# The low part of the weights: a subtraction on VectorE, or a transfer that adds onto the negated high part

## The chip, the cores and the metric

One core of a Trainium2 chip runs the whole program in one launch. The metric is the device time of one execution in microseconds (us). All inputs and outputs lie in HBM.

## What is computed

Three transformer blocks in a row on one sequence of 512 tokens by 1024 channels, in float32. Every block is a mixer and a gated feed-forward of width 2816:

```python
def reference(x, ...):
    x = first_block(x, ...)    # sparse attention (compressed, selected, windowed) + spatial gating, conv feed-forward
    x = second_block(x, ...)   # 2 layers: attention over selected keys + differential attention, swiglu feed-forward
    return third_block(x, ...) # state space branch + delta rule branch, swiglu feed-forward

# the feed-forward of the second block (each layer) and of the third
gate = jnp.einsum('bsd,df->bsf', h2, w_gate[layer])
up = jnp.einsum('bsd,df->bsf', h2, w_up[layer])
x = x + jnp.einsum('bsf,fd->bsd', jax.nn.silu(gate) * up, w_down[layer])
```

Nearly all of the arithmetic is products of activations with weights: the input projections, the output projections and the four feed-forwards (one in the first block, two in the second, one in the third).

## The kernel before

Activations are kept with channels on the 128 partitions and the 512 tokens along the free dimension. A product runs in the matmul format `float32r`, which rounds its operands, so each operand is split into a high part `hi` (the value rounded to `float32r`) and a low part `lo` (the value minus `hi`), and a product is three matmuls: `hi*hi`, `hi*lo`, `lo*hi` (`mm3`, L350 to L352).

Weights come in pieces of 128 partitions by up to 1024 columns (512 KB), 8 tiles of 128 rows of the contraction. `load_piece` (L277) makes one piece: SP issues the load into a raw buffer (`wraw`, `WR` = 4 buffers, L281); ACT copies it with rounding into `whi` (L283); DVE subtracts, `wlo = wraw - whi` (L284). `whi` and `wlo` have `WS` = 3 buffers each. There are 528 pieces in the program: 176 for the gate and up projections (`wup`), 118 for the input projections (`win`), 128 for the down projections (`wdn`: each row of output blocks is one piece of 1024 columns and one of 384, as half of the width is 11 tiles), 56 for the output projections (`wout`, 48 of them 512 columns wide), and some tens of others.

The consumers are `lin_steps` (L299), which takes a piece and issues 24 matmuls (8 tiles by three), each of 128 by 512, and `tok_steps` (L316), which uses the weights as the moving operand. `swiglu` (L1606) makes one tile of 128 channels of the feed-forward: a product with a gate piece, DVE multiplies by the row scale `rbc`, ACT applies Silu, POOL multiplies by `rbc` once more (L1612), a product with an up piece, DVE multiplies the two (L1614) and the result is split again (L291, L292). `out_proj` (L1628) does the output and down projections: per block of 128 channels DVE adds the product to `x`, and ACT and DVE prepare the next normalization.

The framework orders each engine's instructions itself: each engine then runs its own list in order, and tiles with several buffers let a list run ahead as far as buffers come free. SP's list has the loads. POOL's list has elementwise work (L436, L875, L877, L1612 and others), small dependent steps of a triangular system in the third block (L1298, L1303), and six transfers of its own (L1287, L1305, L1310). The rotary embedding (`rope`, L868) exchanges halves by transfers issued from ACT (L874).

The lines that are replaced:

```python
hi, lo = (self.t([P, 1024], tag=tg, bufs=self.WS, dt=F32R, name=tg)[:, :n] for tg in ("whi", "wlo"))
nc.scalar.copy(hi, raw)
nc.vector.tensor_tensor(lo, raw, hi.bitcast(F32), op=ALU.subtract)
```

Of the kernel before, what the change touches and what calls it, by code (L numbers as in the profile page):

```python
# [12 lines left out]
F32 = mybir.dt.float32  # L13
F32R = mybir.dt.float32r
I32 = mybir.dt.int32
AF = mybir.ActivationFunctionType
ALU = mybir.AluOpType
# [3 lines left out]
P = 128  # L21
# [9 lines left out]
# ---------------------------------------------------------------- host layout  # L31
def kpieces(w):
    """[K, M] -> [M/128, 128, K/128 * 128]: one block of columns per row, the contraction on partitions."""
    k, m = w.shape
    a = w.reshape(k // P, P, m // P, P).transpose(2, 1, 0, 3)
    return np.ascontiguousarray(a).reshape(m // P, P, k)


def kmajor(w):
    """[K, N] -> [128, K/128 * N]."""  # L40
    k, n = w.shape
    return np.ascontiguousarray(w.reshape(k // P, P, n).transpose(1, 0, 2)).reshape(P, -1)


def colvec(v):
    """[n * 128] -> [128, n]."""
# [24 lines left out]
def prep(i):  # L71
# [22 lines left out]
    # block 1  # L94
# [43 lines left out]
    # block 2  # L138
# [31 lines left out]
    # block 3  # L170
# [27 lines left out]
# ---------------------------------------------------------------- device code  # L198
class Build:
    def __init__(self, tc, aps, offs, ctx):  # L200
        self.tc, self.nc, self.aps, self.offs = tc, tc.nc, aps, offs
        self.ctx = ctx
        self.uid = 0
        self.sb = ctx.enter_context(tc.tile_pool(name="sb", bufs=1))
# [15 lines left out]
    def t512(self, dt=F32, name="t"):  # L220
        """A [128, 512] slot, taken in program order and given back with free()."""
# [15 lines left out]
    def set_ring(self, **kinds):  # L237
        """Slots that short-lived tiles of a kind go round; 0 gives them back."""
# [13 lines left out]
    def banks(self, **kinds):  # L252
        """Which PSUM banks each kind of product goes round."""
# [22 lines left out]
    # weights: one DMA of [128, n <= 1024], then the exact two-part split  # L276
    def load_piece(self, ap):  # L277
        nc = self.nc
# [7 lines left out]

    def split(self, src, name="s", tiles=None):
        """src [128, n] F32 (SBUF or PSUM) -> hi, lo."""
# [6 lines left out]
    def lin_T(self, ap, xs, tag="mm", piece=None):  # L295
        """ap [128, K] (one block of 128 output rows); xs: list of (hi, lo) per k-tile -> PSUM [128, 512]."""
        return last_of(self.lin_steps(ap, xs, tag, piece))

    def lin_steps(self, ap, xs, tag="mm", piece=None):  # L299
        """lin_T, a k-tile a step; the last step gives the result."""  # L300
# [16 lines left out]
    def tok_steps(self, ap, n, xs, done, wide=1):  # L317
        """ap [128, 8 * n]: tokens on partitions, PSUM [128, n] per token tile to done(tt, ps)."""
# [22 lines left out]
    def scaled(self, o, scale, name):  # L341
        """o * scale in two parts."""
# [4 lines left out]
    def mm3(self, out, w, x, start=True, stop=True):  # L347
        """out (+)= w.T @ x, either operand in two parts."""
# [5 lines left out]
    def scores(self, q, k, qt, masks, mx, sm):  # L354
        """Per half: exp(max - (q.k + mask)) with its row sums; q carries the turned sign."""
# [19 lines left out]
    def turned(self, t, qt):  # L375
        """[queries, keys] -> the blocks of keys on partitions, [128, block, 128 queries]."""
# [10 lines left out]
    def rsqrt(self, y, v, pool=False):  # L387
        """y = v ** -0.5 on small [128, n] tiles; v is SBUF and positive."""
# [17 lines left out]
    def bcast_cols(self, col_of_tt, tag="at"):  # L406
        """[128 tokens, 128 (broadcast)] stationary per token tile -> PSUM [128, 512] rows."""
# [5 lines left out]
    def bcast_pairs(self, cols, tag="at"):  # L413
        """cols [128 tokens, 4, 2] -> PSUM [128 = (2, 64), 512]."""
# [4 lines left out]
    # sums of squares of the residual stream, and what follows from them  # L419
# [19 lines left out]
    def col_sums(self, *accs):  # L439
        """-> PSUM [128 tokens, 4]: sums over the partitions."""  # L440
# [9 lines left out]
    def stat_end(self, st):  # L450
        """-> [128 tokens, 4]: 1 / rms"""
# [13 lines left out]
    def norm_in(self, x, g, hi, lo):  # L465
        """hi + lo = x * g, g a per-partition column."""
# [6 lines left out]
    # ------------------------------------------------------------ block 1  # L473
    def block1(self, x, B, first, g_next, stats):
# [36 lines left out]
        # the overlapping windows of the compressed keys and values, position pairs on partitions  # L511
# [99 lines left out]
        # relative bias strips, sign turned: strip[p, h, c] = -bias[bucket(p + 384 - c)], masked where negative  # L611
# [30 lines left out]
        # the two halves of the spatial gating unit, in parts that go between others  # L642
# [28 lines left out]
        # q / k norms per head  # L671
# [16 lines left out]
        # compressed branch probabilities, transposed to [(r, n), q]  # L688
# [1057 lines left out]
```

## Time and profile before

| | |
|---|---|
| time, median of 2 runs | 3123.56 us (3121.01 and 3126.1) |
| span of the profiled execution | 3123.8 us, 40875 instructions |
| PE busy (matmuls) | 3052.9 us, 98% |
| DVE busy | 1785.8 us, 57% |
| ACT busy | 1231.4 us, 39% |
| POOL busy | 440.5 us, 14% |
| DMA | 299.95 MB, mean 96 GB/s |
| mean granted clock of TensorE | 0.979 of full speed |

The span is the time from the first to the last instruction on the one core, so the profiled execution can be laid beside the median of the runs directly. Engines: PE is TensorE, DVE VectorE, ACT ScalarE, POOL GpSimd, SP the engine that only issues transfers. Matmuls overlap in the array, so that one is listed with 0.39 us although a new one starts every 0.23 us.

### The profile page before, as it was taken

Reading aid. Unit: us, or ns where it says so; the run is one execution under the profiler, and the core shown is the slowest. Engines: PE = TensorE matmul, PEld = TensorE weight load, DVE = VectorE, ACT = ScalarE, POOL = GpSimd, SP = SyncE. Lnnn points to the kernel's source line nnn. Section 1 sums busy time; section 2 is a strip of 40 time slices with the busy share of each in tenths; the row PEclk is TensorE's granted clock in tenths of the full one; section 3 lists DMA queues with packets and bytes.
Section 4 is the critical chain, followed back from the end, with each engine's and each line's share of the span. In section 5 each row is a group of like instructions: output and inputs, shape, how many; then the busy total and the mean of one; then the engine's idle time right before and its main releaser. Section 6 shows DMA issues by size and latency. Waiting matters only on the chain.

```text
span 3123.8 us, 40875 instructions
## 1 busy us (share of the span) xinstructions
PE 3052.9 (98%) x15416; PEld 2437.1 (78%) x15416; DVE 1785.8 (57%) x3400; ACT 1231.4 (39%) x2261; POOL 440.5 (14%) x411
## 2 busy tenths in 40 slices
PE   8999999999999999999999999999999999999998
PEld 6867888887677888887677888877777888888886
DVE  6576655647976333348866333369874665543333
ACT  4365433434455222234454222347543433322222
POOL 0001000011221101121211101110820000211011
PEclk9999999998999999998899999999999999999999
DMA  5402223332212223332213233236434222322322
GB/s 175 125 22 77 90 80 109 99 100 81 74 52 92 95 81 108 97 99 80 72 47 99 93 91 102 79 107 199 155 99 155 85 86 88 108 95 78 110 83 74
DMA packets 124052, 299.95 MB, mean 96 GB/s; under 512 B 28440, under 2 KB 40792, under 8 KB 123856
## 3 DMA queue, kind: packets, MB, share of 16 engines
q1 hardware_dynamic: 115696, 285.79, 29.2%
q10 hardware_dynamic: 7680, 9.97, 1.2%
q8 instruction: 122, 2.00, 0.3%
q0 software_dynamic: 480, 1.57, 0.1%
q14 instruction: 74, 0.61, 0.1%
HBM read 272.52 MB, written 14.79 MB: 92 GB/s over the span
## 4 chain that ended last, share of the span: by engine, by line
PE 87%; DVE 6%; DMA 2%; ACT 2%; POOL 1%; issue 1%; ACTq 1%; SPq 0%; DVEq 0%; POOLq 0%
PE p L350 24%; PE p L351 24%; PE p L352 24%; PE s L362 2%; DMA rope<-rope 2%; PE tr L382 1%; PE ss L444 1%; PE p L333 1%; ACTq L874 1%; DVE isc L925 1%; PE O L1036 1%; PE p L335 1%; PE p L334 1%; POOL rope L877 1%; DVE m L924 1%
## 5 line engine op out<-in xcount | busy, mean ns | idle before, releaser
L350 PE MATMUL p<-xh,whi 128*128 128x512 f32 x2360 | 955.4, 405 | 10.6 <-ACT xh L467 7.2
L283 ACT CAST whi<-wraw 128x1024 fp32r<-128x1024 f32 (+4 forms) x528 | 495.5, 940 | 1181.3 <-PE p L351 851.5
L351 PE MATMUL p<-xl,whi 128*128 128x512 f32 x2360 | 949.4, 402 | 0.5 <-DVE xl L468 0.5
L352 PE MATMUL p<-xh,wlo 128*128 128x512 f32 x2360 | 946.5, 401 | 1.1 <-DMA wraw<-in_b_cw1k 1.1
L284 DVE TENSOR_TENSOR wlo<-wraw,whi 128x1024 fp32r<-128x1024 f32 (+4 forms) x528 | 599.9, 1138 | 325.1 <-ACT whi L283 311.9
L350 PEld LDWEIGHTS p<-xh,whi 128*128 128x128 f32 x2360 | 448.4, 190 | 120.9 <-issue 8.8
L352 PEld LDWEIGHTS p<-xh,wlo 128*128 128x128 f32 x2360 | 447.5, 190 | 107.5 <-issue 4.8
L351 PEld LDWEIGHTS p<-xl,whi 128*128 128x128 f32 x2360 | 448.2, 190 | 103.1 <-issue 5.0
L350 PE MATMUL p<-acth,whi 128*128 128x512 f32 x704 | 277.8, 395 | 0.0
L352 PE MATMUL p<-acth,wlo 128*128 128x512 f32 x704 | 277.7, 394 | 0.0
L351 PE MATMUL p<-actl,whi 128*128 128x512 f32 x704 | 277.5, 394 | 0.0
L1612 POOL TENSOR_TENSOR g<-g,rbc 128x512 f32<-128x512 f32 x66 | 114.0, 1728 | 808.5 <-ACT g L1611 808.5
L436 POOL TENSOR_TENSOR sqacc<-sqacc,sq 128x512 f32<-128x512 f32 x63 | 97.4, 1550 | 777.0 <-ACT sq L434 776.8
L1614 DVE TENSOR_TENSOR g<-g,p 128x512 f32<-128x512 f32 x66 | 45.4, 688 | 238.7 <-PE p L352 238.7
L352 PEld LDWEIGHTS p<-acth,wlo 128*128 128x128 f32 x704 | 132.2, 188 | 31.6
L351 PEld LDWEIGHTS p<-actl,whi 128*128 128x128 f32 x704 | 132.2, 188 | 31.5
L350 PEld LDWEIGHTS p<-acth,whi 128*128 128x128 f32 x704 | 132.2, 188 | 31.3
L1610 DVE TENSOR_TENSOR g<-p,rbc 128x512 f32<-128x512 f32 x66 | 45.7, 692 | 188.1 <-PE p L352 188.1
L369 ACT ACTIVATE stile<-stile,sm 128x128 f32<-128x128 f32 (+3 forms) x192 | 106.8, 557 | 83.3 <-DVE sm L366 72.1
L1634 DVE TENSOR_TENSOR x<-x,p 128x512 f32<-128x512 f32 x96 | 66.0, 688 | 108.1 <-PE p L352 107.9
L333 PE MATMUL p<-whi,xh 128*128 128x256 f32 (+2 forms) x352 | 104.6, 298 | 0.3 <-ACT rope L871 0.3
L334 PE MATMUL p<-wlo,xh 128*128 128x256 f32 (+2 forms) x352 | 102.9, 293 | 0.0
(457 smaller groups left out, 4183.4 us busy)
## 6 DMA issues: line engine op xcount, KB each, us to landing
wraw<-in_b_wup SPq DMA_DIRECT2D x176, 512.0 KB, 3.3
wraw<-in_b_win SPq DMA_DIRECT2D x118, 512.0 KB, 3.6
wraw<-in_b_wdn SPq DMA_DIRECT2D x64, 512.0 KB, 3.5
wraw<-in_b_wout SPq DMA_DIRECT2D x48, 256.0 KB, 2.7
wraw<-in_b_wdn SPq DMA_DIRECT2D x64, 192.0 KB, 2.3
rope<-rope ACTq DMA_DIRECT2D x128, 64.0 KB, 2.3
row<-rows SPq DMA_DIRECT2D x32, 256.0 KB, 4.4
wraw<-in_b_wtC SPq DMA_DIRECT2D x8, 512.0 KB, 4.0
```

The source lines that it names most:

```text
L283: nc.scalar.copy(hi, raw)
L284: nc.vector.tensor_tensor(lo, raw, hi.bitcast(F32), op=ALU.subtract)
L333: mm(ps, xs[k][0][:, ts], wh[:, s], start=k == 0, stop=False)
L334: mm(ps, xs[k][0][:, ts], wl[:, s], start=False, stop=False)
L350: mm(out, w[0], x[0], start=start, stop=False)
L351: mm(out, w[0], x[1], start=False, stop=False)
L352: mm(out, w[1], x[0], start=False, stop=stop)
L362: self.nc.tensor.matmul(out[g][:, :n], q[i][hs, qt * P : n], k[j][hs, :n], start=c == 0, stop=c == 2)
L369: nc.scalar.activation(t[:, :n], t[:, :n], AF.Exp, bias=mx[:, g : g + 1], scale=-1.0, accum_out=sm[:, g : g + 1])
L436: eng.tensor_tensor(accs[i], accs[i], sq, op=ALU.add)
L1612: nc.gpsimd.tensor_tensor(g, g, rbc, op=ALU.mult)
L1634: nc.vector.tensor_tensor(x[m], x[m], ps, op=ALU.add)
```

## The change

`load_piece` gets a second form, and a flag set in the constructor sends all 528 pieces through it. ACT makes `hi` as before. ACT then also writes `-hi` into `lo`. A transfer issued from POOL reads the same weights from HBM a second time and adds them onto `lo`, so that `lo` ends as the weight minus `hi`. DVE has no part in it any more. The raw tile is still loaded, by SP, for `hi` alone. The numbers of buffers stay as they are. The rest of the diff removes comments and docstrings.

```diff
     def __init__(self, tc, aps, offs, ctx):
...
+        self.rmw = True
...
     def load_piece(self, ap):
+        if self.rmw:
+            return self.load_piece_rmw(ap)
         nc = self.nc
...
+    def load_piece_rmw(self, ap):
+
+        nc = self.nc
+        n = ap.shape[1]
+        raw = self.t([P, 1024], tag="wraw", bufs=self.WR, name="wraw")[:, :n]
+        nc.sync.dma_start(raw, ap)
+        hi, lo = (self.t([P, 1024], tag=tg, bufs=self.WS, dt=F32R, name=tg)[:, :n] for tg in ("whi", "wlo"))
+        nc.scalar.copy(hi, raw)
+        nc.scalar.activation(lo, hi.bitcast(F32), AF.Copy, scale=-1.0)
+        nc.gpsimd.dma_start(lo, ap, accum_op=ALU.add)
+        return hi, lo
```

## Rows read from the trace of the kernel before

**Rows 1.** The page's busy times: us, share of the span, instructions.

```profile
PE 3052.9 (98%) x15416; PEld 2437.1 (78%) x15416; DVE 1785.8 (57%) x3400; ACT 1231.4 (39%) x2261; POOL 440.5 (14%) x411
```

**Rows 2.** The page's chain that ended last: shares of the span by engine, by line.

```profile
PE 87%; DVE 6%; DMA 2%; ACT 2%; POOL 1%; issue 1%; ACTq 1%; SPq 0%; DVEq 0%; POOLq 0%
PE p L350 24%; PE p L351 24%; PE p L352 24%; PE s L362 2%; DMA rope<-rope 2%; PE tr L382 1%; PE ss L444 1%; PE p L333 1%; ACTq L874 1%; DVE isc L925 1%; PE O L1036 1%; PE p L335 1%; PE p L334 1%; POOL rope L877 1%; DVE m L924 1%
```

**Rows 3.** Stretches: length, busy PE, PEld, DVE, ACT, POOL, granted clock, DMA share, GB/s.

```profile
0.00:78.00 78.00, 64.84 (x317) 53.95 (x318) 52.07 (x92) 35.72 (x51) 7.66 (x13) 0.91 0.55 175
312.00:690.00 378.00, 378.00 (x1641) 305.32 (x1641) 224.07 (x304) 143.17 (x185) 10.78 (x6) 1.00 0.30 95
703.00:859.00 156.00, 143.09 (x757) 112.83 (x756) 128.92 (x325) 67.91 (x160) 36.55 (x36) 0.88 0.26 77
1406.00:1562.00 156.00, 143.55 (x724) 110.70 (x725) 133.60 (x338) 71.13 (x171) 35.97 (x37) 0.87 0.26 76
2109.00:2187.00 78.00, 76.09 (x357) 61.66 (x356) 70.53 (x161) 60.86 (x93) 0.00 (x0) 1.00 0.66 199
2187.00:2265.00 78.00, 74.87 (x365) 58.23 (x364) 64.23 (x71) 42.50 (x69) 64.03 (x106) 0.98 0.48 155
```

**Rows 4.** The page's groups by line: busy us, mean ns; idle before, releaser.

```profile
L283 ACT CAST whi<-wraw 128x1024 fp32r<-128x1024 f32 (+4 forms) x528 | 495.5, 940 | 1181.3 <-PE p L351 851.5
L284 DVE TENSOR_TENSOR wlo<-wraw,whi 128x1024 fp32r<-128x1024 f32 (+4 forms) x528 | 599.9, 1138 | 325.1 <-ACT whi L283 311.9
```

**Rows 5.** The chain in order of time, pieces of L284: start us, us, what.

```profile
724.01 1.24 DVE wlo L284
...
2296.47 1.13 DVE wlo L284
```

**Rows 6.** Timeline of a swiglu stage: start us, us, engine, line, operation [idle before].

```profile
1908.56 1.05 ACT L283 CAST whi<-wraw 128x1024 fp32r<-128x1024 f32 x1 [3.97 <-PE p L351]
...
1909.52 0.63 ACT L1611 ACTIVATE g<-g 128x512 f32<-128x512 f32 x1
1909.64 1.23 DVE L284 TENSOR_TENSOR wlo<-wraw,whi 128x1024 fp32r<-128x1024 f32 x1 [0.20 <-ACT whi L283]
1910.22 1.80 POOL L1612 TENSOR_TENSOR g<-g,rbc 128x512 f32<-128x512 f32 x1 [9.33 <-ACT g L1611]
1910.89 0.33 SPq L281 DMA_DIRECT2D wraw<-in_b_wup  x1
...
1914.13 1.06 ACT L283 CAST whi<-wraw 128x1024 fp32r<-128x1024 f32 x1 [3.99 <-issue]
1915.11 0.62 ACT L291 CAST acth<-g 128x512 fp32r<-128x512 f32 x1
```

**Rows 7.** The tile `sys`: POOL's own transfers, issue ns min/median/max, and their landing.

```profile
L1287 POOL DMA_DIRECT2D sys<-dAT x2: 547/634/720, 2192.6 to 2193.3; - x2
...
DMA to landing us min/median/max: 2.9/5.3/6.8
```

**Rows 8.** DMA issues of the down projections: count, KB each, us to landing.

```profile
wraw<-in_b_wdn SPq DMA_DIRECT2D x64, 512.0 KB, 3.5
...
wraw<-in_b_wdn SPq DMA_DIRECT2D x64, 192.0 KB, 2.3
```

**Rows 9.** Timeline of ACT in a down projection.

```profile
1171.96 1.05 ACT L283 CAST whi<-wraw 128x1024 fp32r<-128x1024 f32 x1 [1.59 <-PE p L351]
1177.55 0.51 ACT L283 CAST whi<-wraw 128x384 fp32r<-128x384 f32 x1 [4.53 <-PE p L351]
1179.65 1.05 ACT L283 CAST whi<-wraw 128x1024 fp32r<-128x1024 f32 x1 [1.59 <-PE p L351]
```

**Rows 10.** Timeline of ACT in an output projection.

```profile
982.67 0.62 ACT L283 CAST whi<-wraw 128x512 fp32r<-128x512 f32 x1 [0.62 <-ACT sqacc L431]
...
985.45 0.62 ACT L283 CAST whi<-wraw 128x512 fp32r<-128x512 f32 x1 [0.63 <-ACT sq L434]
```

**Rows 11.** Stretches, L284 alone: length, busy DVE, granted clock, DMA share, GB/s.

```profile
703.00:859.00 156.00, 23.56 (x18) 0.88 0.26 77
1406.00:1562.00 156.00, 24.20 (x18) 0.87 0.26 76
```

## The prediction

> **What bounds the kernel now.** I read the page first: busy times, then the chain that ended last. TensorE (PE) is busy for 98% of the span, VectorE (DVE) for 57%, ScalarE (ACT) for 39%, GpSimd (POOL) for 14% [rows 1]. A busy PE may still be waiting inside, so the chain says more: 87% of it is PE, 6% DVE, 2% ACT [rows 2]. Then busy time by stretch: in feed-forward (312 to 690 us; 1010 to 1380, 1720 to 2040 and 2660 to 3124 read alike, 1532 us together) PE has no gap; the slack lies in the attention stretches, where PE falls to 143 of 156 us and the granted clock to 0.88, between the levels of 1.2 and 2.4 GHz [rows 3]. Last, the groups by line and the timelines, for the edited work.
>
> There are 528 pieces of weights, each loaded by SP, rounded by ACT into `whi` (L283, 495.5 us in all) and subtracted on DVE into `wlo` (L284, 599.9 us) [rows 4]. In the chain L284 stands as 14 longer pieces, 21.5 us together: 6 of them in 724 to 814 us (8.2 us), 4 in 1452 to 1475 (5.8), 4 in 2212 to 2297 (7.4); the first and the last stand in [rows 5]. So nearly all of the 600 us is off the path. In feed-forward a piece keeps PE for 5.57 us (one CAST at 1908.56, the next at 1914.13): ACT's CAST starts when PE has read the buffer for the last time [rows 6]. With three buffers, a piece then has two whole pieces of time, 11.14 us, until its first use; the split as it is needs 2.3 of them (CAST to the subtraction's end at 1910.87).
>
> **What the change removes.** 528 subtractions; DVE falls from 1785.8 to about 1186 us. On the path that is the 21.5 us above, **-22 us**. The raw buffer comes free at the CAST's end and not the subtraction's, on which SP's next load follows now (1910.89 us [rows 6]): loads start 1.3 us earlier, worth nothing where pieces wait for PE and not for loads.
>
> **What it adds on ACT.** One scaled copy per piece, SBUF to SBUF. Silu on 128x512 takes 0.63 us, the cast of 128x512 0.62 [rows 6]; the function does not matter, so I price it like the CAST, 1.05 us for 128x1024, 496 us in all. ACT goes from 1231 to 1727 us, 55%. The tightest stretch, 2109 to 2187 us, has 61 of 78 and 12 pieces: 13 more fit [rows 3].
>
> **What it adds on POOL and in the DMA.** 528 accumulating transfers, issued from POOL at 0.55 to 0.72 us each [rows 7], some 320 us of queue. The trace holds no such transfer. The nearest are six plain ones from POOL, 256 KB each: 2.9 to 6.8 us to landing, median 5.3 [rows 7]. On SP 512 KB of `wdn` land 1.2 us after 192 KB [rows 8], so 256 KB more cost 1.0. Lower bound: 2.9 + 1.0 = 3.9 us, the destination's read costing nothing. Middle: 5.3 + 1.0, and 1.9 to read 512 KB of destination too: 8.2. Upper bound: 6.8 + 1.0 and three such reads, 5.7: 13.5. I take 8.2, as an adding transfer must read twice.
>
> The Trainium skill (DMA: Bandwidth & Descriptors, section Anatomy of one DMA — SWDGE (gpsimd) path) gives a transfer from POOL about 2.0 us plus its bytes over 436 GB/s: an estimate of 3.2 us for 512 KB, with which the sum would be that of the hidden case below. For 256 KB that fit gives 2.6 us where the rows have 2.9 to 6.8 [rows 7]: the trace is slower than the page.
>
> **Swiglu stages.** From release to ready: CAST 1.05, one other ACT instruction 0.62, negation 1.05, handoffs 0.2 (as between CAST and subtraction [rows 6]), transfer 8.2: 11.1 us against 11.14, just hidden behind PE's two pieces. With that cover gone, three buffers go round in (5.57 + L)/3 per piece. At every second piece POOL is at `g*rbc`, 1.80 us from 1910.22, 1.66 after the CAST [rows 6]; an issue due 2.9 after the CAST slips 0.55. L = 11.65 gives 5.74: 0.17 us on half of 176 pieces, **+15 us**. In POOL's queue that `g*rbc` stands behind issues that wait for ACT, and DVE's product waits for it, with a piece of slack.
>
> **Down projections.** A big and a small piece alternate, 7.69 us a pair (CAST 1171.96, next 1179.65) [rows 9]. Big: 1.05 + 1.05 + 0.2 + 8.2 = 10.5; small: 0.51 + 0.51 + 0.2 + 5.8 = 7.0 (192 KB, 2 x 1.2 sooner). While three pairs pass, each buffer serves one big and one small: (7.69 + 10.5 + 7.0)/3 = 8.4 us. 64 pairs by 0.71: **+46 us**. Here the cover is gone.
>
> **Output projections** of 512 columns run at 2.78 us a piece (CAST 982.67, next 985.45) [rows 10]. Ready after 3 x 0.62 + 0.2 + 6.3 = 8.4: (2.78 + 8.4)/3 = 3.72; 24 dense pieces, **+23 us**. The other 24, spread through attention, and the 118 `win` pieces I cost at nothing: other matmuls stand between and hide them; dense, they would cost as swiglu's do, 0.09 us each.
>
> **DMA engines.** Feed-forward moves 95 GB/s at a share of 0.30 [rows 3]: 1.67 us of all 16 engines for 512 KB. An accumulating transfer at twice that makes 0.90, which fits. Two stretches don't: 0 to 78 us, 0.55 and 17 pieces, gives 1.25; 2109 to 2187, 0.66 and 12 pieces, 1.17 [rows 3]. The excess by 78 us: 20 + 13, **+33 us**. From 2187 to 2265 POOL is busy for 64 of 78 us with small dependent steps [rows 3]; 11 issues of 0.6 us and some waits among them: **+10 us**.
>
> Sum: 15 + 46 + 23 + 33 + 10 - 22 = +105 us on the profiled span of 3123.8, which lies 0.2 over the median of the runs: **3229 us**, 3.4% slower.
>
> **The rivals.** *Hidden after all*, not slower: transfers land in under 7 us. At the lower bound everything is ready in time (down projections 6.2 + 4.9 = 11.1 against 15.4) and the engines have room: 3124 + 10 - 22 = 3112, up to 3150 at 7 us. For it, POOL transfers of 2.9 us; against, a median of 5.3 with half the bytes and one read [rows 7].
>
> *The DMA engines become the bound*: an accumulating transfer holds them three times as long as a plain one, or longer. Feed-forward needs 0.30 x 4 = 1.2 of them, 1532 x 0.2 = +306 us; the two dense stretches 47 + 34; about 60 more in the third block's projections (a fifth of some 300 us): 3570 us, near 4200 at four times. For it: 199 GB/s already hold 0.66 of the engines [rows 3]; against, no row. It decides from 2.3 times on.
>
> *The subtraction was the brake*, the other side: in the index score stretches (703 to 859, 1406 to 1562 us) L284 takes 48 us [rows 11] of a DVE that is busy for 129 and 134 of 156, and the clock is 0.88 and 0.87 [rows 3]. If those 48 came back, and the clock with them (12.5% of 287 us of PE, 36), 84 us would go: 3040. It decides if DVE's order holds PE there. Against: the chain has 14 us of L284 in them, and ACT's queue and the rope transfers stand in it too [rows 2].
>
> The Trainium skill (SBUF — State Buffer, section Who interferes with whom) has DVE in its two-port modes starve descriptor generation on GpSimd; by it, transfers would land later still wherever DVE copies. No row here prices that.
>
> **How the numbers follow.** Forecast (transfers of 7 to 9.5 us, twice a plain one on the engines; 3150 to 3330): 0.40. Hidden (3102 to 3150): 0.25. Engines bound (3330 and up): 0.28. Brake gone: 0.07. A measurement tells about 2% (62 us) from no change: faster by more 0.07; within, 0.25 and 0.07 of the forecast's low end, 0.32; slower 0.33 + 0.28 = 0.61. The range 3100 to 3600 leaves out the brake and the upper part of the engine case (0.13).
>
> **What would show it.** Right: down projections take 8 to 9 us a pair with PE waiting for POOL's transfers, swiglu pieces stay near 5.6, the transfers land in about 8 us, the DMA share is near 0.9 in feed-forward, and ACT has a new group of 528. Landings under 7 us and pairs at 7.69 make it the hidden case; shares near 1 and swiglu pieces of 6.5 us make it the engines. I am wrong outright if PE idles for ACT, or if an issue keeps POOL for some us.

## The result, and the profile after

The changed kernel takes **3351.67 us** (3350.91 to 3352.43) where the kernel before takes 3123.56: a ratio of **1.0727 [1.0707, 1.0748]**, 228 us slower. The forecast was 3229, in a range of 3100 to 3600. The direction and the range hold; the size does not, it is more than twice the loss that was forecast. The profiled execution after has a span of 3350.6 us, 226.8 over that of before. Line numbers of after stand 15 higher behind the new function: L283 is now L297, L350 to L352 are L365 to L367.

First the page of after: busy times, then the chain that ended last by engine and by line [rows 1, 2].

```profile
PE 3124.9 (93%) x15416; PEld 2467.4 (74%) x15416; DVE 1228.6 (37%) x2872; ACT 1688.8 (50%) x2787; POOL 825.2 (25%) x939
PE 46%; issue 9%; DMA 8%; POOL 4%; DVE 3%; ACT 2%; ACTq 0%; SPq 0%; POOLq 0%; DVEq 0%
PE p L367 13%; PE p L365 13%; PE p L366 13%; DMA wlo<-in_b_wdn 2%; POOL wlo L299 1%; PE s L377 1%; DMA wlo<-in_b_wup 1%; DMA row<-rows 1%; DMA rope<-rope 1%; DMA wlo<-in_b_win 1%; PE tr L397 1%; ACT whi L297 1%; POOL sys L1318 1%; POOL subst L1313 1%; PE O L1051 1%
```

DVE gave up 557 us of work, and the chain no longer runs through PE alone: transfers into `wlo` and their issues stand in it. What the new transfers cost the engines is in the page's queue lines of after (q0 is POOL's queue, q1 SP's: packets, MB, share of 16 engines), and their landing in its DMA issues (count, KB each, us from issue to landing) [rows 7, 8]:

```profile
q0 software_dynamic: 76512, 243.07, 43.7%
q1 hardware_dynamic: 115696, 285.79, 26.1%
wlo<-in_b_wup POOLq DMA_DIRECT2D x176, 512.0 KB, 5.4
wlo<-in_b_win POOLq DMA_DIRECT2D x118, 512.0 KB, 6.1
wlo<-in_b_wdn POOLq DMA_DIRECT2D x64, 512.0 KB, 6.4
wlo<-in_b_wout POOLq DMA_DIRECT2D x48, 256.0 KB, 4.2
```

A byte added holds the engines 43.7/243.07 over 26.1/285.79 = **1.97 times** as long as a byte loaded. That is the "twice" of the forecast. The landings of 512 KB in these groups, 5.4 to 6.4 us in the median, are shorter than its 8.2. So both main inputs of the forecast were right or too gloomy, and the loss is still twice as large. Next the groups by line of after, for the new work and for POOL's old product [rows 4, 6]:

```profile
L297 ACT CAST whi<-wraw 128x1024 fp32r<-128x1024 f32 (+4 forms) x528 | 495.0, 939 | 1014.6 <-PE p L366 975.6
L298 ACT ACTIVATE wlo<-whi 128x1024 fp32r<-128x1024 f32 (+4 forms) x528 | 497.8, 944 | 6.7 <-ACT pts L399 0.7
L299 POOL DMA_DIRECT2D wlo<-in_b_wup x176 | 151.9, 863 | 503.1 <-ACT wlo L298 477.8
L1627 POOL TENSOR_TENSOR g<-g,rbc 128x512 f32<-128x512 f32 x66 | 87.3, 1323 | 232.0 <-ACT g L1626 232.0
```

The negation costs what the CAST costs, as forecast. An issue keeps POOL for 0.86 us, over the 0.55 to 0.72 that were read off POOL's plain transfers [rows 7].

**Where the time went.** The starts of ACT's copies of `rbc` mark the same places in every kernel's trace, so each stage can be laid beside that of before. Four stages by stretch, of before and then of after (columns as in [rows 3]): the mixer of block 1, block 2's first mixer, block 3's input (its conv pieces and triangular solve), and a feed-forward.

```profile
30.60:315.70 285.10, 279.91 (x1848) 222.01 (x1847) 194.91 (x570) 151.00 (x397) 12.37 (x16) 0.96 0.27 84
687.30:1008.20 320.90, 304.17 (x1697) 236.14 (x1696) 237.26 (x588) 151.72 (x354) 67.58 (x63) 0.94 0.25 76
2080.00:2304.00 224.00, 214.35 (x1032) 168.82 (x1031) 186.68 (x335) 136.29 (x217) 72.81 (x111) 0.98 0.51 158
1008.20:1379.50 371.30, 371.30 (x1609) 300.24 (x1608) 144.13 (x178) 106.59 (x139) 48.43 (x28) 1.00 0.31 96
```

```profile
30.60:363.40 332.80, 304.32 (x1864) 236.67 (x1863) 157.92 (x528) 182.93 (x440) 48.02 (x58) 0.90 0.55 126
756.20:1104.00 347.80, 315.61 (x1698) 243.76 (x1697) 196.56 (x544) 184.96 (x398) 103.01 (x107) 0.92 0.54 124
2237.90:2514.90 277.00, 224.75 (x1025) 173.29 (x1024) 142.31 (x302) 163.11 (x245) 84.13 (x142) 0.93 0.74 186
1104.00:1492.30 388.30, 375.84 (x1609) 300.32 (x1608) 64.55 (x102) 174.34 (x215) 100.66 (x104) 1.00 0.82 180
```

The three mixer stages grow by 47.7, 26.9 and 53.0 us, the feed-forward by 17.0. The engines are fullest in the feed-forward (0.82) and it loses least; block 1's mixer, at 0.55, loses nearly three times as much. PE is also busy for longer in the mixers (24, 11 and 10 us, about the same instructions) where its granted clock has sunk from 0.96, 0.94 and 0.98 to 0.90, 0.92 and 0.93, means between the levels of 1.2 and 2.4 GHz: PE waits more there, and part of the loss is matmuls at the lower level. All stages:

| stage | lost, us | forecast |
|---|---|---|
| four feed-forwards (21.2, 17.0, 14.6, 13.3) | 66 | 15 + 46 |
| output projections, blocks 1 and 2 (9.3, 8.2, 9.3) | 27 | 23 |
| block 1 before its output projection | 38 | 20 |
| block 2's two mixers without it | 40 | 0 |
| block 3, 2080 to 2304 us of before | 53 | 13 + 10 |
| block 3's rest | 3 | 0 |
| DVE's relief | in the rows above | -22 |
| sum | 227 | 105 |

**Feed-forward.** In ACT's timeline of after, two CASTs of a swiglu stage, then the CASTs of a down projection; then, from PE's timeline, the first low-part matmul of the big piece whose turn it is [rows 6, 9]:

```profile
2082.90 1.05 ACT L297 CAST whi<-wraw 128x1024 fp32r<-128x1024 f32 x1 [2.97 <-PE p L366]
2088.47 1.05 ACT L297 CAST whi<-wraw 128x1024 fp32r<-128x1024 f32 x1 [3.03 <-PE p L366]
...
505.66 1.05 ACT L297 CAST whi<-wraw 128x1024 fp32r<-128x1024 f32 x1 [1.03 <-PE p L366]
512.22 0.51 ACT L297 CAST whi<-wraw 128x384 fp32r<-128x384 f32 x1 [4.42 <-PE p L366]
514.32 1.05 ACT L297 CAST whi<-wraw 128x1024 fp32r<-128x1024 f32 x1 [1.03 <-PE p L366]
```

```profile
507.03 0.50 PE L367 MATMUL p<-acth,wlo 128*128 128x512 f32 x1 [0.70 <-DMA wlo<-in_b_wdn]
```

Swiglu keeps its old pace, 5.57 us a piece. The pair of the down projection takes 8.66 us where it took 7.69, and PE waits for the landing of `wdn`.

**Block 3.** POOL's timeline of after, behind the negations of pieces 380 and 381 (counted from 0 by their CASTs), which end at 2389.0 and 2393.1 us; in 2386 to 2430 POOL works through the triangular solve, L1313 and L1318:

```profile
2402.64 0.77 POOL L1318 TENSOR_TENSOR sys<-sys,subst 128x55 f32<-128x55 f32 x2
2403.38 0.26 POOL L1313 TENSOR_TENSOR subst<-sys,sys 128x48 f32<-128x48 f32 x1
2403.59 0.82 POOL L299 DMA_DIRECT2D wlo<-in_b_win  x1
2404.20 0.53 POOL L1318 TENSOR_TENSOR sys<-sys,subst 128x48 f32<-128x48 f32 x1
...
2412.54 0.63 POOL L1313 TENSOR_TENSOR subst<-sys,sys 128x255 f32<-128x255 f32 x1
2413.11 0.89 POOL L299 DMA_DIRECT2D wlo<-in_b_win  x1
```

The two issues come 15.6 and 21.1 us after the start of their negations (1.3 us where POOL is free), since POOL takes its instructions in order and the solve stands ahead of them. PE's waits of after, over the whole span (line, what it waited for: us in total, times, longest):

```profile
PE p L367 <- DMA wlo<-in_b_win: 49.9, 14, 12.5
PE p L367 <- DMA wlo<-in_b_wdn: 41.3, 42, 3.2
PE p L367 <- DMA wlo<-in_b_wup: 18.6, 7, 4.4
```

There are many short waits in the down projections and few long ones at the mixers' `win` pieces. Added up over the stages, PE's waits that end with a low part come to 48 us in the feed-forwards and 111 us in the mixers; before, it waited for none.

### The profile page after: what moved, and what is told of

It is laid out like the page before. It is cut to its first block, busy times and chain, and to the rows that moved or that the text cites. A ratio compares the mean times of both kernels' runs of the same rounds, so it can differ in the third digit from the quotient of the medians.

```text
span 3350.6 us, 41864 instructions
## 1 busy us (share of the span) xinstructions
PE 3124.9 (93%) x15416; PEld 2467.4 (74%) x15416; DVE 1228.6 (37%) x2872; ACT 1688.8 (50%) x2787; POOL 825.2 (25%) x939
## 3 DMA queue, kind: packets, MB, share of 16 engines
q0 software_dynamic: 76512, 243.07, 43.7%
q1 hardware_dynamic: 115696, 285.79, 26.1%
## 4 chain that ended last, share of the span: by engine, by line
PE 46%; issue 9%; DMA 8%; POOL 4%; DVE 3%; ACT 2%; ACTq 0%; SPq 0%; POOLq 0%; DVEq 0%
PE p L367 13%; PE p L365 13%; PE p L366 13%; DMA wlo<-in_b_wdn 2%; POOL wlo L299 1%; PE s L377 1%; DMA wlo<-in_b_wup 1%; DMA row<-rows 1%; DMA rope<-rope 1%; DMA wlo<-in_b_win 1%; PE tr L397 1%; ACT whi L297 1%; POOL sys L1318 1%; POOL subst L1313 1%; PE O L1051 1%
## 5 line engine op out<-in xcount | busy, mean ns | idle before, releaser
L367 PE MATMUL p<-xh,wlo 128*128 128x512 f32 x2360 | 953.5, 405 | 68.6 <-DMA wlo<-in_b_win 49.9
L297 ACT CAST whi<-wraw 128x1024 fp32r<-128x1024 f32 (+4 forms) x528 | 495.0, 939 | 1014.6 <-PE p L366 975.6
L365 PE MATMUL p<-xh,whi 128*128 128x512 f32 x2360 | 961.6, 407 | 11.6 <-ACT xh L482 7.0
L367 PEld LDWEIGHTS p<-xh,wlo 128*128 128x128 f32 x2360 | 452.2, 192 | 182.4 <-DMA wlo<-in_b_win 55.8
L365 PEld LDWEIGHTS p<-xh,whi 128*128 128x128 f32 x2360 | 452.3, 192 | 122.3 <-issue 9.2
L298 ACT ACTIVATE wlo<-whi 128x1024 fp32r<-128x1024 f32 (+4 forms) x528 | 497.8, 944 | 6.7 <-ACT pts L399 0.7
L367 PE MATMUL p<-acth,wlo 128*128 128x512 f32 x704 | 284.2, 404 | 41.4 <-DMA wlo<-in_b_wdn 41.3
L365 PE MATMUL p<-acth,whi 128*128 128x512 f32 x704 | 279.6, 397 | 0.0
L299 POOL DMA_DIRECT2D wlo<-in_b_wup x176 | 151.9, 863 | 503.1 <-ACT wlo L298 477.8
L299 POOL DMA_DIRECT2D wlo<-in_b_win x118 | 102.9, 875 | 505.5 <-ACT wlo L298 448.4
L299 POOL DMA_DIRECT2D wlo<-in_b_wdn x128 | 110.3, 862 | 394.7 <-ACT wlo L298 392.9
L367 PEld LDWEIGHTS p<-acth,wlo 128*128 128x128 f32 x704 | 133.3, 189 | 91.1 <-DMA wlo<-in_b_wdn 61.3
L365 PEld LDWEIGHTS p<-acth,whi 128*128 128x128 f32 x704 | 133.5, 190 | 29.8
L1627 POOL TENSOR_TENSOR g<-g,rbc 128x512 f32<-128x512 f32 x66 | 87.3, 1323 | 232.0 <-ACT g L1626 232.0
L349 PE MATMUL p<-wlo,xh 128*128 128x256 f32 (+2 forms) x352 | 111.7, 319 | 34.0 <-DMA wlo<-in_b_wtA 12.8
```

What stands on the lines that cost most here:

```text
L298: nc.scalar.activation(lo, hi.bitcast(F32), AF.Copy, scale=-1.0)
L299: nc.gpsimd.dma_start(lo, ap, accum_op=ALU.add)
L349: mm(ps, xs[k][0][:, ts], wl[:, s], start=False, stop=False)
L365: mm(out, w[0], x[0], start=start, stop=False)
L367: mm(out, w[1], x[0], start=False, stop=stop)
L1627: nc.gpsimd.tensor_tensor(g, g, rbc, op=ALU.mult)
```

## The experiments

Three theories stood at the start: A, the low part comes late; B, the doubled traffic holds the DMA engines; C, ACT's program order. All diffs are against the changed kernel's `load_piece_rmw`.

**Without the transfer.** The line of the transfer is left out.

```
-        nc.gpsimd.dma_start(lo, ap, accum_op=ALU.add)
```

> ACT writes both parts as in the changed kernel (rounding, then the negation), DVE does no subtraction, and the accumulating transfer is left out, so that the low part stays the negated high part. What is left of the change is the 528 negations on ACT and the 600 us taken off DVE. If the loss of 228 us comes from the transfer (its landing time or its traffic), this runs in 3095 to 3125 us: nothing lost, at most the 22 us of subtractions gained that stood in the chain. If ACT's longer list is the cause, the attention stages and the third block keep their loss of some 90 us: 3190 or more.

Measured: 3105.51 us, 0.9943 [0.9914, 0.9971]. ACT's 528 negations cost nothing that shows, and DVE's relief is real: 18 us (9 to 27 by the interval), and 25 in the profiled execution, where the forecast took 22 from the chain. All the loss hangs on the transfer.

**The transfer beside the computation.** DVE's subtraction is back; the adds go into two spare tiles that nobody reads, and the raw tiles go from four to two to make room.

```
+        nc.vector.tensor_tensor(lo, raw, hi.bitcast(F32), op=ALU.subtract)
+        nc.gpsimd.dma_start(self.side[self.turn][:, :n], ap, accum_op=ALU.add)
```

> The split of the kernel before (rounding on ACT, subtraction on DVE), and beside it the same 528 accumulating transfers from POOL, onto two buffers that nobody reads; to make room the raw tiles have 2 buffers instead of 4. The traffic and POOL's issues are those of the changed kernel, but no matmul waits for them. If lateness of the low part is the cause: 3124 to 3150 us. If the doubled traffic slows every other transfer (rows of the third block, rope, weights): 3230 or more, with waits for plain transfers.

Measured: 3821.2 us, 1.2221 [1.2149, 1.2293]: much slower than the change that it should explain. The page's DMA line, in tenths of 40 slices:

```profile
DMA  9999999998999999972323222222254342232322
```

And one of PE's waits (us in total, times, longest):

```profile
PE ss L465 <- POOL sqacc L457: 195.5, 4, 106.0
```

Little paced these transfers but each other. They ran back to back through the first half and held the engines full, POOL's own work queued behind their issues, and once they were through, the rest ran at the old pace. The run says what full engines cost (about 700 us in some 1700), not what the change's traffic costs.

**Four buffers.** Four `whi`/`wlo` pairs for three, paid for with two raw tiles for four.

```
-b.TMP, b.WR, b.WS = 4, 4, 3
+b.TMP, b.WR, b.WS = 4, 2, 4
```

> The changed kernel with 4 buffers instead of 3 for the high and the low part, and 2 instead of 4 for the raw tile. The transfers, the negations and the traffic stay; each piece has one more piece of time. If lateness is the cause, the down projections return to 7.7 us a pair (-60 us) and the output projections to 2.8 (-25), and much of the start and the attention stages comes back: 3150 to 3230 us. If traffic or ACT's list is the cause: 3320 or more.

Measured: 3265.69 us, 1.0444 [1.0395, 1.0493]. The feed-forwards lose 3 us for 66, the mixers still 139 for 161. The adding transfers move what they moved. So the feed-forwards' loss is lateness against the round of three buffers and not full engines. For the mixers the run decides less: PE still waits there for a low part for 71 us in all (111 in the change), and what two raw tiles for four cost by themselves no run shows.

**Negation first.** In program order ACT negates the raw tile ahead of the CAST, so that the transfer can be issued about 1 us sooner.

```
+        nc.scalar.activation(lo, raw, AF.Copy, scale=-1.0)
+        nc.gpsimd.dma_start(lo, ap, accum_op=ALU.add)
         nc.scalar.copy(hi, raw)
```

> The changed kernel with the negation taken straight from the raw tile and ahead of the rounding copy (the rounding of the negative is the negative of the rounded), so that POOL's transfer can be issued some 1.05 us (512 columns: 0.6 us) sooner. If lateness is the cause, a pair in the down projections shortens by half of that, as the big piece takes the buffer that a small one frees: 8.65 to 8.1 us, -34 us; output projections -8; with the start and the attention stages 3260 to 3300 us. If traffic is the cause: 3345 to 3355. If ACT's list is: no more than 15 us better.

Measured: 3349.23 us, 1.0711 [1.0663, 1.0759], no gain. The page's landings, to be held against 5.4, 6.1 and 6.4 of the change:

```profile
wlo<-in_b_wup POOLq DMA_DIRECT2D x176, 512.0 KB, 7.7
wlo<-in_b_win POOLq DMA_DIRECT2D x118, 512.0 KB, 7.7
wlo<-in_b_wdn POOLq DMA_DIRECT2D x64, 512.0 KB, 7.4
```

The edit did not do all that it was meant to: the framework orders ACT's list itself, and in the trace the negation leads the CAST at only 109 of the 528 pieces, at none of the down projections. There the issue comes 2.10 us after the CAST's start in the median, for 2.23 in the change, so the run is no test of an earlier issue for them. In the swiglu stages it comes at 2.31 us for 2.91, and what was won was lost in flight. The raw tile is now held until the negation has read it, so SP's next load goes out 0.27 us ahead of POOL's transfer (1.83 us in the change), and both land later: the loads of `wup` after 5.8 us for 3.4, the adds after 7.7 for 5.4.

**Adds that nobody waits for.** DVE subtracts; afterwards the transfer adds onto the raw tile, in the change's place and rhythm.

```
+        nc.vector.tensor_tensor(lo, raw, hi.bitcast(F32), op=ALU.subtract)
+        nc.gpsimd.dma_start(raw, ap, accum_op=ALU.add)
```

> The split of the kernel before, and beside it the same 528 accumulating transfers, each onto the raw tile of its own piece after the subtraction has read it. Traffic, POOL's issues and their pace are those of the changed kernel, but no matmul waits for a transfer; what is slowed by traffic or by POOL's list still is, and a raw buffer comes free only when the transfer has landed. If the lateness of the low part is the whole loss: 3124 to 3150 us. If POOL's list and the traffic cost the mixers their part: 3200 to 3280, with feed-forward at its old pace.

Measured: 3268.55 us, 1.0471 [1.0413, 1.0528]. The feed-forwards lose 5 us, the mixers 141. Here no matmul waits for an add, so the traffic and the held raw tiles cost the mixers nearly as much as the change does, by another way: a raw tile comes free only when its add has landed, ACT's CASTs wait for the loads behind it (118 us in all, for 8 before and 5 in the change), and PE waits for ACT's and DVE's work behind the CASTs. The run shows that the adds can cost this much without lateness of the low part, not that they do so in the change, and it does not tell the traffic from the held tiles.

**A plain transfer.** The same transfer without the addition.

```
-        nc.gpsimd.dma_start(lo, ap, accum_op=ALU.add)
+        nc.gpsimd.dma_start(lo, ap)
```

> The changed kernel with the addition taken out of POOL's transfer, which then writes the weights over the negated part (the low part is the whole weight). The order on ACT and POOL, the issues and the waits stay; each transfer reads once and not twice. If the landing time and the hold on the DMA engines are what counts, landings fall from 5.4 to about 4 us, the down projections return to 7.7 us a pair (-60 us) and the whole to 3220 to 3270. If the lists of ACT and POOL are what counts, the mixers keep their loss of some 160 us: 3290 or more.

Measured: 3207.45 us, 1.0275 [1.0228, 1.0322]. The feed-forwards lose 10 us, the mixers 72. Queue and landings on its page:

```profile
q0 software_dynamic: 76512, 243.07, 26.0%
wlo<-in_b_wup POOLq DMA_DIRECT2D x176, 512.0 KB, 3.7
wlo<-in_b_wdn POOLq DMA_DIRECT2D x64, 512.0 KB, 4.4
```

The addition by itself is worth 142 us (228 less 86). The 86 that are left should not be there by the forecast's working: landings near its lower bound of 3.9 us were to have everything ready in time.

**Feed-forwards alone.** The transfer for `wup` and `wdn`, the subtraction for all others.

```
-        if self.rmw:
+        if ap.tensor.name.endswith(("wup", "wdn")):
```

> The transfer only for the gate, up and down pieces (304 of 528); the mixers' pieces keep the subtraction. If the parts add up, feed-forward loses what it loses in the changed kernel (66 us: 0 in swiglu, some 8 in each half of a down projection) and the mixers nothing: 3185 to 3200 us. If feed-forward loses by traffic that the mixers leave behind, less; if by something of its own, the same 66.

Measured: 3204.25 us, 1.0265 [1.0217, 1.0313]. The feed-forwards lose 64 us, as in the whole change, the mixers 16 in all. The stages' losses add up.

**Negation on DVE.**

```
-        nc.scalar.activation(lo, hi.bitcast(F32), AF.Copy, scale=-1.0)
+        nc.vector.tensor_scalar(lo, hi.bitcast(F32), -1.0, None, op0=ALU.mult)
```

> The changed kernel with the negation on DVE instead of ACT. The transfer, its issue from POOL and the traffic stay. If ACT's list holds the negations back in the mixers (4 to 7 us after the rounding in the third block), the third block and the attention stages get 30 to 60 us back: 3290 to 3320. If the transfer's landing alone counts: 3335 to 3355, the same as the change.

Measured: 3362.56 us, 1.0772 [1.0680, 1.0864]: no better. In its trace, the longer of two executions (3372.77 and 3352.34 us), block 3 loses 17 us less and block 2's mixers more than 20 each more. With the first run this leaves theory C without support for the kernel as a whole.

**A transfer of one thirty-second.**

```
-        nc.gpsimd.dma_start(lo, ap, accum_op=ALU.add)
+        nc.gpsimd.dma_start(lo[:, :32], ap[:, :32], accum_op=ALU.add)
```

> The changed kernel with its adding transfer cut to the first 32 of up to 1024 columns, so 1/32 of the added bytes of a big piece; the other columns of the low part stay the negated high part (part of the computation is left out). ACT's negation, POOL's issue and the matmul's wait for a landing all stay as in the change. Theory traffic (the loss is the time and the hold of the added bytes): both the 66 us of the four feed-forwards and most of the mixers' 161 us go, 3105 to 3150 us. Theory lists (a wait in ACT's or POOL's program order ahead of the transfer, whatever it moves): the mixers keep what the plain transfer kept, about 72 us, 3180 to 3200 us. In between, about 20 us left in block 3's pieces 376 to 384 alone (POOL's triangular steps ahead of the issue) and nothing elsewhere would give 3125 to 3145.

Measured: 3183.45 us, 1.0194 [1.0173, 1.0215]. The feed-forwards lose nothing; the mixers keep 15 (block 1), 6, 6 and 26 us (block 3), in the range of the theory on lists, with almost no bytes moved. What those microseconds are, lists or the fixed time of a transfer, this run left open; the touch below tells. PE's waits of its trace in block 3 (2101 to 2360 us):

```profile
PE p L367 <- DMA wlo<-in_b_win: 19.0, 6, 6.7
```

And the landing of the tile `wlo`, over the whole span:

```profile
DMA to landing us min/median/max: 2.2/2.3/7.1
```

**The add from the raw tile.** The weights are not read from the chip's memory a second time.

```
-        nc.gpsimd.dma_start(lo, ap, accum_op=ALU.add)
+        nc.gpsimd.dma_start(lo, raw, accum_op=ALU.add)
```

> The changed kernel whose adding transfer reads the raw weights from the tile that SyncE's load has already filled, in place of reading them from the chip's memory a second time; bytes moved by the DMA engines, lists and waits are otherwise the same (the raw tile is held until the transfer lands). Theory engines (the 16 DMA engines' time per byte is the price): no better than the change, 3330 to 3380 us, queue share of the adding transfers still about 44%. Theory memory reads (the second read of the weights is the price): nearer to the plain transfer, 3200 to 3260 us, share of that queue about 26 to 35%.

Measured: 3266.63 us, 1.0468 [1.0445, 1.0492]. The feed-forwards lose 23 us, the mixers 118. The page's queue and memory lines:

```profile
q0 software_dynamic: 76512, 243.07, 41.4%
HBM read 272.52 MB, written 14.79 MB: 88 GB/s over the span
```

Neither theory came out whole: the engines are held nearly as long (1352 us for 1464), and yet 85 us are back, and the time is some 7 us above the range of the theory on memory reads. The time on the engines alone does not set the loss. That the second read of the memory has a price of its own fits this run, which holds the raw tiles longer and is still faster; in which way that read costs time it does not show.

**Subtraction on POOL.** No second transfer; POOL subtracts for the mixers of blocks 1 and 2, DVE for the feed-forwards and block 3.

```
+        nc.gpsimd.tensor_tensor(lo, raw, hi.bitcast(F32), op=ALU.subtract)
```

> The kernel before with the subtraction of blocks 1 and 2's mixers and output projections put on POOL, DVE keeping that of the four feed-forwards and of block 3; no second transfer. If the gain that was read for the relieved DVE (25 us in all with the transfer left out, 17 of it before block 3) comes from DVE's list alone: 3105 to 3118 us. If a low part that POOL makes later than DVE takes the gain back: 3124 to 3170 us.

Measured: 3218.01 us, 1.0308 [1.0286, 1.0331], worse than both expectations. By engine and shape, POOL's group in its trace:

```profile
L299 POOL TENSOR_TENSOR wlo<-wraw,whi 128x1024 fp32r<-128x1024 f32 x74 | 179.1, 2433 | 191.0 <-ACT whi L298 168.7 <-PE p L367 8.9 <-issue 5.9
```

The mixers of blocks 1 and 2 lose 26, 34 and 27 us, the feed-forwards nothing, and PE's waits name `wlo` for some 10 us only; the longest total is `s` for ACT's `kh`, 20.4. In these stretches DVE took 1.34 us for what POOL does in 2.43. While POOL subtracts, DVE's other work is slower too: the same 1642 instructions in the two blocks' mixers take 714 us, for 632 before and 635 in the change. One of them, in block 2's first mixer, before and in this run:

```profile
L941 DVE SCALAR_TENSOR_TENSOR isc<-relu,iw,isc 128x256 f32<-128x256 f32 x7 | 4.4, 627 | 0.1
L956 DVE SCALAR_TENSOR_TENSOR isc<-relu,iw,isc 128x256 f32<-128x256 f32 x7 | 8.4, 1207 | 0.7 <-ACT relu L955 0.3
```

So block 2's mixers lose as much as with the change, and block 1's about half, without any added transfer. Whether by the later low part, POOL's longer queue or the slower DVE the run does not tell; as DVE's other work is not slower in the change, it is no model of it.

**Block 3 spared.** Subtraction for `b3_win` alone.

```
-        if self.rmw:
+        if not ap.tensor.name.endswith("b3_win"):
```

> The changed kernel with DVE's subtraction kept for block 3's input pieces only. If the stretches' losses stand by themselves (as the feed-forwards' 64 of 66 us did), the 53 us lost between 2080 and 2304 go and nothing else: 3295 to 3310 us. If a loss spared in one stretch is paid in the next, because the engines' queues carry over, 3320 us or more.

Measured: 3294.51 us, 1.0552 [1.0534, 1.0570]. Block 3's 53 us are gone (it gains 4), and nothing else moves by more than 6 us.

**A touch for the transfer.** POOL copies one column where it issued the transfer.

```
-        nc.gpsimd.dma_start(lo, ap, accum_op=ALU.add)
+        nc.gpsimd.tensor_copy(lo[:, :1], raw[:, :1])
```

> The changed kernel with no second transfer: where POOL issued it, POOL copies one column of 128 values (the rest of the low part stays the negated high part; part of the computation is left out). Matmuls still wait for ACT's negation and for POOL to reach that place in its list, but for no transfer. Theory lists (the 55 us that were left with a transfer of 1/32 are the wait in ACT's and POOL's order): about the same, 3165 to 3185 us, block 3 still 20 us or more. Theory landing (they are the 2.3 us and more that even a small transfer takes to land, with its 0.86 us issue): back to what no transfer gave, 3100 to 3135 us. In between, block 3 alone keeping 15 to 25 us (POOL's triangular steps) and the rest gone: 3120 to 3140 us.

Measured: 3135.31 us, 1.0036 [1.0024, 1.0048]. The time lies in the range of the third reading, and block 3's input loses 9 us against the kernel before, some 20 more than without any transfer. PE's waits for the touch:

```profile
PE p L367 <- POOL wlo L299: 18.2, 3, 16.3
```

One wait of 16.3 us, in block 3 behind the solve, is most of it. Against no transfer at all (-18 us) the wait for POOL's place in the order costs 29 us (11 + 18). From here to the thirty-second, another 50 (61 - 11): the price of issue and landing with almost no bytes.

**The solve off POOL**, with the change and, as a control, with DVE's subtraction.

```
-                nc.gpsimd.tensor_tensor(
+                nc.vector.tensor_tensor(
                     pr, r16(sa[k // 16])[:, k % 16, i0:i1].unsqueeze(2).to_broadcast([P, n, k + 1]),
...
-                nc.gpsimd.tensor_tensor(dst, dst, pr, op=ALU.subtract)
+                nc.vector.tensor_tensor(dst, dst, pr, op=ALU.subtract)
```

> The whole change, with the products and subtractions of block 3's triangular solve moved from POOL to DVE, so that they no longer stand ahead of the issues of pieces 379 to 384 on POOL. If those issues, 9 to 22 us late, cost about 20 of block 3's 53 us: 3322 to 3338 us. If block 3's loss is the landings' under the engines' load, whoever issues: 3345 to 3358 us.

> The kernel before (DVE's subtraction, no second transfer) with the same move of the triangular solve from POOL to DVE: what the move costs or gains by itself, against which the run with the whole change is read. 3110 to 3125 us if DVE has room for it in block 3 (it is 83 per cent busy between 2080 and 2304 us before), up to 3150 us if it hasn't.

Measured: with the change 3327.9 us, 1.0660 [1.0627, 1.0692]; the control 3131.04, 1.0024 [1.0010, 1.0038]. Block 3's input loses 32 us for 53, and the move by itself gains nothing there (its loss against the kernel before is within 1 us of none). POOL's order ahead of the issues is 21 us of block 3; the other 32 stay wherever the solve runs.

Laid in a row, by the medians' ratios (times 3123.6): without the transfer -18 us; with POOL's place in the order kept +11; with a transfer of almost nothing +61; with a plain one +86; with the adding one +227. Each of these has an interval of 4 to 15 us either side, so the differences are rough. No version tried with a second transfer comes down to the kernel before, and the one that beats it leaves out part of the low part.

## Why the forecast was too small

**DVE's relief, -22.** This held: -18 by the medians, -25 in the profiled execution. That the subtraction was the brake (84 us) fell with the same run.

**ACT's negation.** This held: 0.944 us a piece against the CAST's 0.939, and no loss by itself.

**The transfer's price.** Twice a plain one on the engines: 1.97, held. The landing of 8.2 us was too long; 5.4 to 6.4 at 512 KB. The Trainium skill (DMA: Bandwidth & Descriptors, section Anatomy of one DMA — SWDGE (gpsimd) path) gave an estimate of 3.2 us for 512 KB and the sum of the hidden case. The quickest plain transfer of the run without the addition took 3.27, but the medians are 3.7 to 4.4, and the adding ones take longer still, so the measurement decides against it here. The Trainium skill's 2.0 us of fixed time, in the same section, are close to the 2.2 that the smallest took. The upper bound of 13.5 was not foolish for the dense stretches: the longest landing is 12.9.

**Swiglu, +15.** Measured 0. From CAST to landing a `wup` piece takes 8.35 us in the median of 176, under the 11.14 that two pieces give.

**Down projections, +46.** Measured 66 with the turns to the next stage; pairs of 8.66 us against 8.4. The forecast has two errors of opposite sign (and a rounding: 64 pairs by 0.71 are 45 us, not 46). The landing was too long. And the round was averaged over big and small pieces, (7.69 + 10.5 + 7.0)/3, where with three buffers a big piece always takes the buffer that a small one left. From there to its own turn there is one pair of PE's work, so the pair takes (7.69 + L)/2, with L that of the big piece alone. L is 9.54 in the median of 64, which gives 8.62. With the forecast's own 10.5 the right round would have given 9.1 and 90 us.

**Output projections, +23.** Measured 27, and the agreement is luck. The dense pieces did not go over to the forecast's 3.72 us: in block 2's first mixer the CASTs start at 1067.5, 1070.3, 1073.1, 1075.9 and 1080.3 us, so they keep 2.8 us but for the last step. PE's waits there (1055 to 1104 us of after):

```profile
PE p L367 <- DMA wlo<-in_b_wup: 4.4, 1, 4.4
PE p L367 <- DMA wlo<-in_b_wout: 2.1, 2, 1.3
```

The longer wait is for the first piece of the next feed-forward, and the other two stretches read alike (3.7 us each).

**The mixers' other pieces, nothing. This is the step that failed**: "The other 24, spread through attention, and the 118 `win` pieces I cost at nothing: other matmuls stand between and hide them". Over 130 us of the 227 lie in the stages of these pieces, where the forecast had 43. In the trace of after a `win` piece takes 10.3 us from CAST to landing in the median of 118, up to 28.6; in the kernel before the low part of these pieces was there after 2.9 in the median, at most 11.1. I had taken the cover from busy shares and never measured it at one piece. The runs show three parts, none of them in the sum for these pieces, save 10 us for POOL's list. The first is POOL's order ahead of the issue: 29 us, some 20 of it block 3's solve (21 by its own pair of runs). The second is the price of any transfer, even of 16 KB with a landing of 2.3 us: 50. The third is the size: in the feed-forwards all of the size's cost is lateness, as four buffers took it away; in the mixers it is some 17 us for plain bytes (72 against 55) and some 90 more for adding (161 against 72). PE's waits for a low part in the mixers, added up by trace, are 23 us with the touch, 36 with the thirty-second, 60 with the plain transfer and 111 with the adding one. So 51 of those 90 us stand in the trace as waits for a later low part. Whether it is late by the transfer's own length or by others in its way, and where the other 40 lie, is open. The adds onto the raw tile cost the mixers 141 us with no matmul waiting for them, so adds can cost that without lateness of the low part; the add from the raw tile gave back 43 of the mixers' 161 at nearly the same hold on the engines, so the engines' time is not the whole account.

**DMA-dense stretches, +33, and POOL's list, +10.** The start lost 27 us by piece 16 (75.7 us in the kernel before) against 20; the forecast's own numbers, 0.55 and 17 pieces at 3.34 us, give 1.28 for its 1.25, so 22. From 2080 to 2304 us 53 were lost against 23. Both reasons stood in the forecast by name. POOL's list was priced too low: of 11 issues "of 0.6 us and some waits" single ones were held up to 21.7 us, and the list cost 21 us for 10. The other 32 us, for 13, did not come by engines that are over full: in the trace of after they are busy for 0.85 at the start (0 to 103 us) and 0.84 ahead of the solve (2268 to 2386 us), while PE waits for landings.

**The clock.** The sum had no term for it. PE is busy 72 us longer than before (3124.9 against 3052.9), and the granted clock is lower in the mixers of blocks 1 and 2 and in block 3's input; PE idles there for 147 us in all, for 48 before. By the granted clock of the two traces PE is busy at the lower level, 1.2 GHz, for 114 us before and for 211 after. Matmuls of 128x512 back to back start every 0.43 us there and every 0.23 us at the upper level, which makes some 44 of the 72 us the clock's, an estimate from these rows; the rest they do not explain. It is no term to be added: the stages' losses above contain it.

**The rivals.** The condition of the hidden case, landings under 7 us, came true in the medians of the four largest groups, and its result did not: it looked at the feed-forwards' cover only. Its small piece, ready after 4.9 us, should be 3.9 by the forecast's own terms (0.51 + 0.51 + 0.2 + 2.7), which changes nothing in it. The engines as the bound did not come: 0.81 to 0.82 of them are busy in the feed-forwards of blocks 1 and 2, under the 0.9 of the forecast. That transfers land later where DVE copies has one run beside it, the negation on DVE: an issue keeps POOL for 0.866 us in the median as for 0.862 in the change, and the landings of `wup`, `win` and `wdn` go from 5.4, 6.1 and 6.4 us to 5.6, 7.0 and 7.0. Whether DVE's copies cause that is not shown.

## What to carry to other kernels

Price an added transfer at the pieces with the shortest cover, not at the most frequent ones: measure from release to first use at such a piece, and add what stands ahead of the issue in its queue. Two experiments split such a price quickly: the same transfer with almost no bytes, and a touch in its place. For rotating buffers of unequal pieces, follow which piece takes which buffer; an average over them hides the one that is late.

## What the runs showed of the hardware

An adding transfer occupies POOL for 0.86 us at its issue even when it moves 32 columns (0.863 us in the mean of the `wup` pieces, whole or cut), a plain one of the same pieces for 0.55. A plain transfer from POOL holds the engines 1.1 times as long per byte as SP's loads (26.0/243.07 against 27.7/285.79, the queue line below), an adding one 1.97 times. An add with its source on the chip holds them nearly as long, and still the kernel is 85 us faster.

POOL's product of 128x512 in the swiglu stages took 1728 ns beside DVE's subtractions and takes 1323 in the change; without the transfer, where POOL's list is otherwise as it was, it takes 1297. Where DVE subtracts again for the feed-forwards, in the run with POOL's subtraction for the mixers, it is 1728 as before. In the same run DVE's other instructions in the mixers take 714 us beside POOL's subtractions, for 632 before. The group in the run without the transfer:

```profile
L1626 POOL TENSOR_TENSOR g<-g,rbc 128x512 f32<-128x512 f32 x66 | 85.6, 1297 | 837.2 <-ACT g L1625 837.2
```

And SP's line in the run with the plain transfer, from which the 27.7 comes:

```profile
q1 hardware_dynamic: 115696, 285.79, 27.7%
```
